# Moving a background scan forward in a two-layer kernel: first stage by K with eight output tiles, squares on ScalarE, outputs grouped by four

## The chip, the cores and the metric

The kernel runs on one core of a Trainium2 chip. The metric is the device time of one execution in microseconds (us), lower is better; the median of several executions is compared. The core has a matrix engine (TensorE, PE in the profile; PEld is its weight load), VectorE (DVE), ScalarE (ACT), GpSimd (POOL), and SyncE (SP), which issues most of the DMAs.

## The reference

Two layers run on 256 tokens of width 2048, in fp32. What the change touches lies in the first layer, which is cut to its core here:

```python
h = rmsnorm(x, norm_g)
v, bg, cg, za, u, zb, ga, gb = split(h @ w_in)      # 4 x 2048, 2 x 1024, 2 x 2048 columns
ya = (bg * causal_depthwise_conv(cg * v, conv_w) * silu(za)) @ w_out_a
yb = gelu(s5_scan(u))                               # 64 groups of 16 channels, 64 complex states each
yb = yb * sigmoid(yb @ w_glu + b_glu)
yb = (yb * silu(zb)) @ w_out_b
x1 = x + (sigmoid(ga) * ya + sigmoid(gb) * yb) @ w_o

def s5_scan(u):
    lam_bar = exp(lam * dt)                         # complex, |lam_bar| and an angle
    bu = einsum(((lam_bar - 1) / lam) * b, u)
    h[t] = lam_bar * h[t-1] + bu[t]                 # along the 256 tokens
    return real(einsum(c, h)) + d_skip * u
```

The second layer (attention beside an RWKV mix, then a gated feed-forward block) is the same in both kernels.

## The kernel before

**Matrix products.** Activations lie transposed, channels on the 128 partitions and 256 tokens along the free axis. A value that is multiplied is kept as a high part (fp32r) and a low part. `gemm` makes one output tile of 128 channels; for each block of 128 along K (a *K step*) it issues two matmuls, wh (high weights) on the high and low part together, 128x512, and wl (low weights) on the high part, 128x256. Weights come in blocks of 512 KB, one block for 8 K steps: SP loads `wf`, ACT casts `wh` (`_cast_to`), DVE subtracts `wl` (`_split_to`), each with four buffers and up to three blocks ahead (`sub`). So every 8 K steps need one `wh` on ACT and one `wl` on DVE, in whatever the stage does besides.

**Order.** The program is scheduled by hand: each engine runs its instructions in the order in which the code writes them. `gemm` calls `tick` after every K step; `tick` runs the background generators that `later` registered, and the number that a generator yields (or its default) is how many K steps pass until its next piece is written. `flush` writes out what is left of them. A time in the code is therefore a number of K steps, and a piece that is not ready when its engine comes to it stops that engine.

**Stages of the first layer, in K steps.** u takes K steps 0 to 128; the loop over f (v, cg, bg and za, four tiles for each of 16 f) goes to 1152; `ya_out`, which multiplies by `w_out_a`, to 1408; zb, ga and gb to 2048. Then the generator of the scan must be done (`flush(s5)`), and `w_glu` follows. The tile `vs` is evicted when K step 144 has ended, the first after u, and the tile `yb` is multiplied first when K step 2048 has ended.

**u.** `_block1` scales x by `norm_g` into X (ACT the high part, DVE the low part) two K blocks at a time, POOL squares x into `sq`. The first four output tiles go through K together, two K blocks per tile; the other four follow one after the other. `first_norm` adds up the squares (POOL and DVE), and `rstd` makes R, the reciprocal norm along the tokens, by a matmul with ones (`st`), some small DVE and ACT work and another matmul (`al`). `u_out` waits for R, evicts u times R, and splits it into `uh`, which goes to DRAM (`s5u`).

**The scan.** `s5` is a generator that starts after u: `s5_prep` makes small parameters (tile `sm`, mostly 128x32 on DVE and POOL), the block-diagonal matrices `bd`, and their transposes `bt` on PE; `s5_base` makes a table of the first 32 powers on POOL; and then 32 steps follow, each for two groups of channels. A step multiplies u (`bu`, two matmuls), turns it by the conjugate angles of its table (DVE products from PSUM, POOL sums), runs two real scans on DVE (line 670), turns it back (one product on POOL, one on DVE, two sums on POOL), and gives h. Beside it `s5_table` doubles the table of the next step three times (32, 64, 128 columns), one ACT and two DVE instructions each. The output y of step k is multiplied when step k+1 issues its `bu`: two fp32 matmuls of 32 output rows for the channels of that step, which go to one quarter of the bank y. After four steps y is evicted by `gelu`. In K steps, `bu` and y stand at 559, 601, 643 and so on, about 43.5 apart, to 1952, and y comes 7 K steps after the last instruction of its h.

Of the kernel before, what the change touches and what calls it, by code (L numbers as in the profile page):

```python
# [86 lines left out]
class K:  # L87
# [473 lines left out]
    def s5_base(self):  # L561
# [7 lines left out]
        for j in range(5):  # L569
# [3 lines left out]
            for i in range(2):  # L573
                self.tt(A[:, i], T[:, i, :, 0:n], pc, eng=g)
                yield 1 + j
                self.tt(B[:, 1 - i], T[:, i, :, 0:n], ps, eng=g)
                yield 1 + j
            self.tt(T[:, 0, :, n:2 * n], A[:, 0], B[:, 0], ALU.subtract, g)
            yield 1 + j
            self.tt(T[:, 1, :, n:2 * n], A[:, 1], B[:, 1], ALU.add, g)  # L580
            yield 1 + j

    def s5_table(self, k, T, w):

        base = self.flat(self.base).rearrange("p (i k t) -> p i k t", i=2, k=32)
        self.act(T[:, :, 0:32], base[:, :, k])
        for j in (5, 6, 7):
            n = 1 << j
            wv = w[:, 0:2 * n].rearrange("p (i t) -> p i t", i=2)
# [24 lines left out]
    def s5(self, U):  # L614

        nc, g = self.nc, self.nc.gpsimd
        for n in self.s5_prep():
            yield n or 9
        yield from self.s5_base()
        self.stg = self.flat(self.chunk(F32R, "stg")).rearrange("p (h i j t) -> p h i j t", h=2, i=2, j=2)  # L620
# [3 lines left out]
        two = lambda a: a[:, None, :].broadcast_to([128, 2, 256])  # L624
        ring = [c[:, 512 * i:512 * i + 512]
                for c in (self.flat(x) for x in (self.chunk(name="s5"), self.chunk(name="s5"), self.s5c)) for i in range(4)]
        m1, m2, x, s, d1, d2, w = ring[:7]
        tabs = {k: v2(ring[7 + k]) for k in range(2)}
        yield from self.s5_table(0, tabs[0], w)
        yp = {}  # L630
        for k in range(32 + 1):
            tab = iter(()) if k + 1 >= 32 else self.s5_table(k + 1, tabs[(k + 1) % 2], w)
            T, h = tabs[k % 2], ring[9 + k % 2]
            if k < 32:
                if k % 2 == 0:
# [7 lines left out]
            if k >= 1:  # L643
                a = k - 1
                q, j = divmod(a, 4)
                if j == 0:
                    yp[q] = self.pb("y")
                ha = ring[9 + a % 2]
                o = yp[q][32 * j:32 * j + 32, 0:256]
                self.mm(o, cb[:, 0, a], ha[:, 0:256], True, False)  # L650
                self.mm(o, cb[:, 1, a], ha[:, 256:512], False, True)
                if j == 3:
                    yield
                    self.later(self.gelu(q, yp.pop(q), U))
            if k == 32:
                break
            next(tab, None)
            yield
            p = v2(p[:])
            self.tt(v2(m1), p, two(T[:, 0]))  # L660
            self.tt(v2(m2), p, two(T[:, 1]))
            next(tab, None)
            yield
# [11 lines left out]
            self.tt(v2(d1), v2(s), two(T[:, 0]), eng=g)  # L675
# [3 lines left out]
            self.tt(h[:, 0:256], d1[:, 0:256], d2[:, 256:512], ALU.subtract, g)  # L679
            self.tt(h[:, 256:512], d1[:, 256:512], d2[:, 0:256], ALU.add, g)  # L680
# [14 lines left out]
    def u_out(self, p, dst, hl):  # L695
        yield from self.wait_r()
        yield from self.take(p, dst, self.R[:])
# [3 lines left out]
    def conv_out(self, f, cv, o):  # L701
        self.ts(o[:], cv[:, 0:256], self.vec("conv0", f))
# [70 lines left out]
    def _block1(self):  # L773
# [3 lines left out]
        sqs = [self.chunk(name="sq") for _ in range(2)]  # L777
# [5 lines left out]
        def scale(b):  # L783
            for k in (2 * b, 2 * b + 1):
                src = xin[k // 8][:, k % 8]
                for _ in self.scaled(X[k], src, self.vec("norm_g", k)):
                    pass
                self.tt(sqs[k // 8][:, k % 8], src, src, eng=g)

        for b in range(4):  # L790
            load(b)
# [6 lines left out]
        s, t = sqs  # L798
        self.r_ready = False

        def first_norm():
            yield 48
            for q in sqs:
                self.tt(q[:, 0:4], q[:, 0:4], q[:, 4:8], ALU.add, g)
                self.tt(q[:, 0:2], q[:, 0:2], q[:, 2:4], ALU.add, g)
            yield 16
            self.tt(s[:, 0:2], s[:, 0:2], t[:, 0:2], ALU.add)
            self.tt(self.sums[0], s[:, 0], s[:, 1], ALU.add)
            yield 6
            self.act(self.eps[:, 2:3], self.eps[:, 0:1], AF.Sqrt)  # L810
            yield 6
# [20 lines left out]
        self.s5u, self.s5b = ([self.dram.tile([128, 8, 256], F32, name=f"s5{n}{i}") for i in range(2)] for n in "ub")  # L832
# [4 lines left out]
        self.gelus = 0  # L837
        s5 = self.later(self.s5(U), ev=False, default=7)
# [724 lines left out]
def layout(a):  # L1563
# [10 lines left out]
    first = r["w_in"][:8].reshape(4, 2, 128, 4, 256)  # L1574
    r["w_in"][:8] = first.transpose(1, 3, 2, 0, 4).reshape(8, 128, 1024)
# [78 lines left out]
```

## Time and profile before

| | before |
|---|---|
| median of 3 runs | 2263.07 us (2261.43 to 2264.4) |
| profiled execution | 2257.78 us, its span 2256.0 us |
| PE busy | 2183.2 us, 97% of the span |
| DVE busy | 1714.4 us, 76% |
| ACT busy | 1093.1 us, 48% |
| POOL busy | 660.1 us, 29% |

The span goes from the first to the last instruction of the profiled execution. Busy is what an engine's own instructions cover; a busy PE may still run below its best rate. All times of rows are counted from the start of the span.

### The profile page before, as it was taken

The numbers are of one execution on the slowest core, as the hardware profiler recorded it, in microseconds if no ns is written. First come the engines' busy times: TensorE is split into PE (matmuls) and PEld (weight loads), VectorE is DVE, ScalarE is ACT, GpSimd is POOL, SyncE is SP. The second block draws the span as 40 slices with busy tenths as digits, with TensorE's granted clock in tenths as the row PEclk, the third lists the DMA queues.
The fourth block names the chain that finished last, engine by engine and source line by source line (L and its number), as shares of the span: only waits on it lengthen the run. The fifth ranks groups of instructions, "written<-read, shape, count | busy, mean of one in ns | idle before, by whom it ended". The sixth has DMA issues, their size and how long they took to land.

```text
span 2256.0 us, 37791 instructions
## 1 busy us (share of the span) xinstructions
PE 2183.2 (97%) x14500; PEld 1897.6 (84%) x14500; DVE 1714.4 (76%) x2607; ACT 1093.1 (48%) x1742; POOL 660.1 (29%) x744
## 2 busy tenths in 40 slices
PE   7999999999999999999998999999999999999997
PEld 6888777778878888899998888988888888888886
DVE  7888999988899979776797888886666555666554
ACT  5544444444445465554543454454444334444443
POOL 4345555545565312323431000411111001111111
PEclk9999999999999999999999999999999999999998
DMA  6766555557566556766546533666666666666663
GB/s 215 259 215 198 165 166 165 163 180 205 173 193 193 179 182 204 225 219 195 168 142 191 167 116 128 205 185 187 187 184 184 189 184 187 187 186 187 187 186 112
DMA packets 139537, 414.11 MB, mean 184 GB/s; under 512 B 27148, under 2 KB 43837, under 8 KB 137693
## 3 DMA queue, kind: packets, MB, share of 16 engines
q1 hardware_dynamic: 130236, 398.89, 57.2%
q0 software_dynamic: 8256, 10.49, 1.8%
q8 instruction: 114, 1.87, 0.3%
q10 hardware_dynamic: 864, 2.33, 0.3%
q14 instruction: 67, 0.54, 0.1%
HBM read 397.99 MB, written 15.75 MB: 183 GB/s over the span
## 4 chain that ended last, share of the span: by engine, by line
PE 75%; DVE 14%; DMA 3%; issue 3%; POOL 3%; ACT 1%; SPq 0%; DVEq 0%; POOLq 0%; ACTq 0%
PE acc L145 71%; DVE wl L132 5%; POOL s L132 2%; DVE s L139 2%; PE y L145 1%; DVE s L670 1%; DVE s L132 1%; ACT wh L142 1%; DMA wf<-z_in 1%; DMA a_dram<-gm 1%; DMA wf<-w_in 1%; DVE att L132 0%; DVE gb L132 0%; DVE z L132 0%; DMA gb<-a_dram 0%
## 5 line engine op out<-in xcount | busy, mean ns | idle before, releaser
L145 PE MATMUL acc<-X,wh 128*128 128x512 f32 (+1 forms) x4576 | 1397.6, 368 | 6.3 <-ACT wh L142 6.3
L132 DVE TENSOR_TENSOR wl<-wf,wh 128x1024 fp32r<-128x1024 f32 (+1 forms) x711 | 917.7, 1294 | 276.0 <-ACT wh L142 271.5
L145 PE MATMUL acc<-X,wl 128*128 128x256 f32 x3888 | 1064.9, 282 | 5.6 <-DVE wl L132 5.5
L142 ACT ACTIVATE wh<-wf 128x1024 fp32r<-128x1024 f32 (+1 forms) x711 | 748.9, 1055 | 541.6 <-PE acc L145 378.8
L145 PEld LDWEIGHTS acc<-X,wh 128*128 128x128 f32 x4576 | 811.7, 190 | 151.7 <-issue 12.8
L145 PEld LDWEIGHTS acc<-X,wl 128*128 128x128 f32 x3888 | 739.9, 190 | 27.5 <-DVE wl L132 7.5
L145 PE MATMUL acc<-s,wh 128*128 128x512 f32 (+1 forms) x726 | 246.8, 392 | 0.0
L132 POOL TENSOR_TENSOR z<-z,R 128x256 f32<-128x256 f32 x44 | 59.0, 1342 | 523.3 <-ACT sg L142 523.3
L145 PE MATMUL acc<-s,wl 128*128 128x256 f32 x704 | 192.7, 281 | 0.0
L145 PEld LDWEIGHTS acc<-s,wh 128*128 128x128 f32 x726 | 133.0, 188 | 28.9
L132 POOL TENSOR_TENSOR s<-s 128x256 f32<-128x256 f32 x128 | 114.2, 911 | 110.7 <-DVE s L132 105.1
L145 PEld LDWEIGHTS acc<-s,wl 128*128 128x128 f32 x704 | 133.0, 189 | 3.2
L132 POOL TENSOR_TENSOR sum<-sum,sq 128x256 f32<-128x256 f32 x59 | 56.1, 960 | 200.3 <-ACT sq L142 200.3
L139 DVE SCALAR_TENSOR_TENSOR s<-s,s 128x32 f32<-128x32 f32 (+2 forms) x192 | 111.9, 622 | 0.0
L142 ACT ACTIVATE z<-acc 128x256 f32<-128x256 f32 x100 | 38.2, 382 | 126.8 <-PE acc L145 126.6
L145 PE MATMUL acc<-ya,wh 128*128 128x512 f32 x256 | 90.8, 402 | 0.1
L145 PE MATMUL acc<-m,wh 128*128 128x512 f32 x256 | 89.4, 399 | 0.0
L132 DVE TENSOR_TENSOR h<-acc,h 128x256 f32<-128x256 f32 x111 | 46.9, 422 | 43.9 <-PE acc L145 41.1
L132 DVE TENSOR_TENSOR z<-acc,z 128x256 f32<-128x256 f32 x100 | 41.9, 419 | 45.2 <-ACT z L142 45.2
L132 POOL TENSOR_TENSOR bv<-bv,gs 128x128 f32<-128x128 f32 x16 | 13.3, 834 | 209.1 <-DVE bv L139 209.0
L145 PE MATMUL acc<-ya,wl 128*128 128x256 f32 x256 | 70.1, 283 | 0.4 <-ACT ya L142 0.4
L145 PE MATMUL acc<-m,wl 128*128 128x256 f32 x256 | 69.3, 281 | 0.0
(285 smaller groups left out, 2540.5 us busy)
## 6 DMA issues: line engine op xcount, KB each, us to landing
wf<-gate_up SPq DMA_DIRECT2D x176, 512.0 KB, 3.5
wf<-w_in SPq DMA_DIRECT2D x143, 512.0 KB, 4.0
wf<-down SPq DMA_DIRECT2D x88, 512.0 KB, 3.7
wf<-w_in_g SPq DMA_DIRECT2D x80, 512.0 KB, 3.7
wf<-z_in SPq DMA_DIRECT2D x54, 512.0 KB, 3.7
wf<-w_out_a SPq DMA_DIRECT2D x32, 512.0 KB, 3.9
wf<-w_o SPq DMA_DIRECT2D x32, 512.0 KB, 3.9
wf<-qk_in SPq DMA_DIRECT2D x32, 512.0 KB, 4.2
```

The costliest lines, as they stand in the source:

```text
L132: (eng or self.nc.vector).tensor_tensor(out=out, in0=a, in1=b, op=op)
L139: self.nc.vector.scalar_tensor_tensor(out=out, in0=a, scalar=s, in1=b, op0=op0, op1=op1)
L142: self.nc.scalar.activation(out=out, in_=a, func=f, **k)
L145: self.nc.tensor.matmul(out, l, r, start=start, stop=stop)
L670: nc.vector.tensor_tensor_scan(out=s[:, 256 * i:256 * i + 256], data0=r, data1=x[:, 256 * i:256 * i + 256], initial=0.0, op0=ALU.mult, op1 ...
```

## The change

1. **u by K.** All eight output tiles go through K blocks 0 to 11 together, one K step each, in eight PSUM banks; K blocks 12 to 15 then follow tile by tile. X is scaled one K block at a time. The first blocks of `w_in` are laid out for this order.
2. **Squares on ACT.** A generator makes each square on ACT and POOL adds it to `sums[0]`; the 16 squares on POOL and the trees of sums are gone. R is made later (`first_norm` waits 100 K steps).
3. **u unscaled.** `u_out` evicts u before R is there and multiplies by R in place afterwards.
4. **The scan starts in the u stage,** at K step 24 instead of 128, with 8 rather than 7 K steps between pieces, and a preparation of 4 rather than 9; after `s5_base` it waits until u is in DRAM. Its `bu` now stand at K step 279, 327 and so on, 48.25 apart, to 1774.
5. **`s5_table`** makes two products on ACT and two sums on POOL for each doubling; DVE has no part in it.
6. **Outputs by four.** h is kept in a ring of four, and `outputs` multiplies four steps at once: eight matmuls, the four quarters of the bank in turn, 24 K steps after the last instruction of the fourth h.
7. `conv_out` makes its first product on ACT instead of DVE.

The core of the diff:

```diff
     def s5_table(self, k, T, w):
-            self.act(wv, T[:, :, 0:n], scale=self.pw[:, 1, j, k:k + 1])
-            yield
-            pc = self.pw[:, 0, j, k:k + 1]
-            self.stt(T[:, 0, n:2 * n], T[:, 0, 0:n], pc, wv[:, 1], ALU.mult, ALU.subtract)
-            self.stt(T[:, 1, n:2 * n], T[:, 1, 0:n], pc, wv[:, 0], ALU.mult, ALU.add)
+            self.act(A, T[:, :, 0:n], scale=self.pw[:, 0, j, k:k + 1])
+            self.act(B, T[:, :, 0:n], scale=self.pw[:, 1, j, k:k + 1])
+            yield
+            self.tt(T[:, 0, n:2 * n], A[:, 0], B[:, 1], ALU.subtract, self.nc.gpsimd)
+            self.tt(T[:, 1, n:2 * n], A[:, 1], B[:, 0], ALU.add, self.nc.gpsimd)
             yield
...
     def s5(self, U):
         for n in self.s5_prep():
-            yield n or 9
+            yield n or 4
         yield from self.s5_base()
+        while not self.u_stored:
+            yield 1
...
+        def outputs(q):
+            y = self.pb("y")
+            for i in range(2):
+                for j in range(4):
+                    self.mm(y[32 * j:32 * j + 32, 0:256], cb[:, i, 4 * q + j], hs[j][:, 256 * i:256 * i + 256],
+                            i == 0, i == 1)
+            return y
...
-            if k >= 1:
-                a = k - 1
-                q, j = divmod(a, 4)
-                if j == 0:
-                    yp[q] = self.pb("y")
-                ha = ring[9 + a % 2]
-                o = yp[q][32 * j:32 * j + 32, 0:256]
-                self.mm(o, cb[:, 0, a], ha[:, 0:256], True, False)
-                self.mm(o, cb[:, 1, a], ha[:, 256:512], False, True)
...
+            if k and k % 4 == 0:
+                y = outputs(k // 4 - 1)
+                yield 1
+                self.later(self.gelu(k // 4 - 1, y, U))
...
     def u_out(self, p, dst, hl):
+        yield from self.take(p, dst)
+        yield
         yield from self.wait_r()
-        yield from self.take(p, dst, self.R[:])
+        self.tt(dst, dst, self.R[:])
...
     def conv_out(self, f, cv, o):
-        self.ts(o[:], cv[:, 0:256], self.vec("conv0", f))
+        self.act(o[:], cv[:, 0:256], scale=self.vec("conv0", f))
...
+        def squares():
+            for k in range(16):
+                sq = self.square(0, xin[k // 8][:, k % 8], first=k == 0)
+                yield 2
+                self.add_square(sq)
+                yield 4
...
         def first_norm():
-            yield 48
-            for q in sqs:
-                self.tt(q[:, 0:4], q[:, 0:4], q[:, 4:8], ALU.add, g)
-                self.tt(q[:, 0:2], q[:, 0:2], q[:, 2:4], ALU.add, g)
-            yield 16
-            self.tt(s[:, 0:2], s[:, 0:2], t[:, 0:2], ALU.add)
-            self.tt(self.sums[0], s[:, 0], s[:, 1], ALU.add)
-            yield 6
+            yield 100
...
-        ps = [self.acc() for _ in range(3)] + [self.pb("acc")]
-        for b in range(8):
-            if b < 5:
-                scale(b + 3)
-            part = [self.gemm(X[2 * b:2 * b + 2], p, b == 0, b == 7) for p in ps]
+        ps = [self.pb("acc") if q in (0, 2, 4, 6, 7) else self.acc() for q in range(8)]
+        self.later(squares(), ev=False)
+        for k in range(12):
+            if k + 5 < 16:
+                scale(k + 5)
+            if k == 3:
+                s5 = self.later(self.s5(U), ev=False, default=8)
+            for p in ps:
+                self.gemm(X[k:k + 1], p, k == 0, False)
         for q in range(8):
-            p = part[q] if q < 4 else self.gemm(X, self.pb("acc") if q in (4, 5) else None)
+            p = self.gemm(X[12:16], ps[q], False, True)
             self.later(self.u_out(p, U[:, q], [c[:, q] for c in uh]))
```

**PE, the outputs.** This is how PE's order of before reads where a step of the scan issues `bu` and the y of the step ahead of it (`s` is the scratch that holds h, `cbd` the matrix c); the rows around are those of a projection:

```order
L145 MATMUL acc_2380<-X_101,wl_2297 128x256
L145 MATMUL acc_2380<-X_102,wh_2316 128x512
L145 MATMUL acc_2380<-X_102,wl_2335 128x256
L145 MATMUL bu_2412<-stg_1991 128x256 x2
L145 MATMUL y_2415<-s_639,cbd_645 32x256 x2
```

In the changed kernel the y of four steps stand together, without a `bu` beside them; the first two rows of y are the four products of the real part, one for each quarter, and the next two those of the imaginary part:

```order
L145 MATMUL acc_2151<-X_99,wl_2065 128x256
L145 MATMUL y_2173<-s_1110,cbd_272 32x256
L145 MATMUL y_2173<-s_266,cbd_272 32x256 x3
L145 MATMUL y_2173<-s_1110,cbd_272 32x256
L145 MATMUL y_2173<-s_266,cbd_272 32x256 x3
L145 MATMUL acc_2151<-X_99,wh_2054 128x512
```

The y moved away from the `bu` and behind more K steps, and its neighbours now write different quarters of the bank.

**POOL, the squares.** This is the start of POOL's order before, where it squares x and adds up in trees:

```order
L132 TENSOR_TENSOR sq_98<-x_96 128x256 x8
L132 TENSOR_TENSOR sq_99<-x_97 128x256 x8
L132 TENSOR_TENSOR sq_98<-sq_98 128x1024
L132 TENSOR_TENSOR sq_98<-sq_98 128x512
L132 TENSOR_TENSOR sq_99<-sq_99 128x1024
L132 TENSOR_TENSOR sq_99<-sq_99 128x512
```

In the changed kernel the last sums of squares stand on POOL behind the small operations of `s5_prep` (`sm`, and `s` for the powers kept in a chunk of that name):

```order
L132 TENSOR_TENSOR sm_264<-s_266 128x32 x3
L132 TENSOR_TENSOR s_266<-sm_264 128x32 x2
L132 TENSOR_TENSOR sum_88<-sum_88,sq_574 128x256
L132 TENSOR_TENSOR sum_88<-sum_88,sq_600 128x256
L132 TENSOR_TENSOR sm_264<-sm_264 128x32 x8
L132 TENSOR_TENSOR sm_264<-braw_269,sm_264 128x512 x2
```

The squares left POOL, and what makes R ready there now stands in one row with the scan's preparation.

**DVE, the chain that makes R.** Before, it stands among the weights and the last scaled X, in the middle of the u stage:

```order
L132 TENSOR_TENSOR wl_429<-wf_332,wh_416 128x1024
L136 TENSOR_SCALAR rs_437<-st_426 128x2
L331 RECIPROCAL rs_437<-rs_437 128x2
L139 SCALAR_TENSOR_TENSOR rs_437<-rs_437 128x2
L132 TENSOR_TENSOR rs_437<-rs_437 128x2
L139 SCALAR_TENSOR_TENSOR rt<-rs_437 128x2
L136 TENSOR_SCALAR dg_456<-ident,rt 128x128 x2
L132 TENSOR_TENSOR wl_465<-wf_358,wh_445 128x1024
L360 COPY R<-al_455 128x256
```

In the changed kernel it stands at the end of that stage. The evictions of u (`u`), the matrices of the scan (`sm` from `braw`, `bd`), the weights (`wl`) and the chain that makes R (`rs`, `rt`, `dg`) follow one another; the second matmul of R needs the last row:

```order
L132 TENSOR_TENSOR u_159<-acc_166,u_159 128x256
L132 TENSOR_TENSOR sm_264<-braw_269,sm_264 128x512
L132 TENSOR_TENSOR u_159<-acc_167,u_159 128x256
L136 TENSOR_SCALAR rs_679<-st_668 128x2
L132 TENSOR_TENSOR bd_267<-sm_264 64x32x16 x2
L132 TENSOR_TENSOR wl_689<-wf_534,wh_672 128x1024
L132 TENSOR_TENSOR u_159<-acc_168,u_159 128x256
L331 RECIPROCAL rs_679<-rs_679 128x2
L139 SCALAR_TENSOR_TENSOR rs_679<-rs_679 128x2
L132 TENSOR_TENSOR rs_679<-rs_679 128x2
L139 SCALAR_TENSOR_TENSOR rt<-rs_679 128x2
L136 TENSOR_SCALAR dg_703<-ident,rt 128x128 x2
```

The chain moved behind work of the scan that DVE came to only in the loop over f before.

## Rows read from the trace of the kernel before

**Rows 1.** Windows by stage: us long; busy us (instructions) by engine; TensorE clock; DMA.

```profile
core 0: us, PE busy (x) PEld busy (x) DVE busy (x) ACT busy (x) POOL busy (x), PEclk, DMA share, GB/s
...
217.00:472.00 255.00, 238.93 (x1293) 196.04 (x1292) 239.61 (x351) 114.35 (x190) 129.52 (x141) 0.98 0.56 166
571.00:824.00 253.00, 246.58 (x1357) 204.62 (x1356) 225.50 (x302) 127.95 (x218) 124.09 (x135) 0.99 0.62 183
```

**Rows 2.** Tile vs: its first line, which begins when K step 144 ends.

```profile
L142 ACT ACTIVATE vs<-acc x16: 363/380/387, 69.0 to 448.9; 128x256 f32<-128x256 f32 x16
```

**Rows 3.** Tile yb: its first line, which begins when K step 2048 ends.

```profile
L145 PEld LDWEIGHTS acc<-yb,wh x64: 187/188/192, 824.1 to 846.6; 128*128 128x128 f32 x64
```

**Rows 4.** Chain of waits, its longest piece: start, us, what.

```profile
1502.32 736.38 PE acc L145 x4190
```

**Rows 5.** PE timeline around one scan step: start, us, instruction.

```profile
510.31 0.41 PE L145 MATMUL bu<-stg 96*128 96x256 f32 x2
510.64 1.05 PE L145 MATMUL y<-s,cbd 128*32 128x256 f32 x4
511.62 0.50 PE L145 MATMUL acc<-ya,wh 128*128 128x512 f32 x1
```

**Rows 6.** Waits from 217 to 824 us: us in total, times, longest.

```profile
PEld y L145 <- POOL s L132: 38.1, 39, 3.1
...
PE y L145 <- POOL s L132: 22.1, 17, 2.9
```

**Rows 7.** PE timeline of the second layer, matmuls in small tiles of the array.

```profile
1308.33 0.65 PE L145 MATMUL y<-ch,gm 64*32 64x64 f32 x32
1308.91 0.39 PE L145 MATMUL acc<-X,wh 128*128 128x256 f32 x1
```

**Rows 8.** Groups of DVE by form, 217 to 790 us: busy us, mean ns, idle before.

```profile
L670 DVE TENSOR_TENSOR_SCAN s<-s5r,s 128x256 f32<-128x256 f32 x64 | 48.2, 793 | 0.6 <-POOL s L132 0.6
L139 DVE SCALAR_TENSOR_TENSOR s<-s,s 128x128 f32<-128x128 f32 x62 | 43.5, 739 | 0.0
L132 DVE TENSOR_TENSOR s<-bu,s 128x512 f32<-128x512 f32 x64 | 41.0, 681 | 0.0
L139 DVE SCALAR_TENSOR_TENSOR s<-s,s 128x64 f32<-128x64 f32 x62 | 35.4, 610 | 0.0
L139 DVE SCALAR_TENSOR_TENSOR s<-s,s 128x32 f32<-128x32 f32 x62 | 30.5, 533 | 0.0
L132 DVE TENSOR_TENSOR s<-s,s 128x512 f32<-128x512 f32 x32 | 23.4, 732 | 0.0
```

**Rows 9.** Groups of POOL by form, 69 to 217 us, three of s5_base.

```profile
L132 POOL TENSOR_TENSOR ab<-base,s 128x128 f32<-128x128 f32 x4 | 2.6, 662 | 0.1
...
L132 POOL TENSOR_TENSOR ab<-base,s 128x32 f32<-128x32 f32 x4 | 1.2, 331 | 0.0
...
L132 POOL TENSOR_TENSOR ab<-base,s 128x64 f32<-128x64 f32 x4 | 1.1, 312 | 0.1
```

**Rows 10.** Timeline of one POOL product beside DVE, and the same product later.

```profile
489.11 3.11 POOL L132 TENSOR_TENSOR s<-s,s 128x512 f32<-128x512 f32 x1 [4.97 <-DVE s L670]
...
489.85 1.22 DVE L132 TENSOR_TENSOR wl<-wf,wh 128x1024 fp32r<-128x1024 f32 x1
...
505.01 1.39 POOL L132 TENSOR_TENSOR s<-s,s 128x512 f32<-128x512 f32 x1 [3.54 <-ACT wh L142]
```

**Rows 11.** Window of the u stage, all engines.

```profile
0.00:69.00 69.00, 57.10 (x297) 48.74 (x298) 54.33 (x86) 37.23 (x60) 25.95 (x30) 0.98 0.67 221
```

**Rows 12.** Windows of sm (DVE, POOL), bd (PE, PEld, DVE, POOL), sq (five engines); cbd's group.

```profile
60.00:217.00 157.00, 18.99 (x75) 22.05 (x51) 1.00 0.69 226
60.00:217.00 157.00, 2.40 (x16) 1.90 (x16) 3.28 (x4) 1.87 (x2) 1.00 0.69 226
0.00:69.00 69.00, 0.00 (x0) 0.00 (x0) 1.11 (x2) 0.00 (x0) 22.06 (x20) 0.98 0.67 221
...
L136 DVE TENSOR_SCALAR cbd<-cbd 128x1024 f32<-128x1024 f32 x1 | 1.2, 1250 | 0.0
```

**Rows 13.** PE's waits from 0 to 60 us: us in total, times, longest.

```profile
PE acc L145 <- DVE wl L132: 5.5, 3, 3.1
```

More of the change, by code (lines that the diff above doesn't have):

```diff
@@ L624, in s5 @@
         two = lambda a: a[:, None, :].broadcast_to([128, 2, 256])
+        s5 = [self.chunk(name="s5") for _ in range(2)]
         ring = [c[:, 512 * i:512 * i + 512]
-                for c in (self.flat(x) for x in (self.chunk(name="s5"), self.chunk(name="s5"), self.s5c)) for i in range(4)]
-        m1, m2, x, s, d1, d2, w = ring[:7]
-        tabs = {k: v2(ring[7 + k]) for k in range(2)}
-        yield from self.s5_table(0, tabs[0], w)
-        yp = {}
+                for c in (self.flat(x) for x in (s5[0], s5[1], self.s5c)) for i in range(4)]
+        m1, m2, d2 = ring[:3]
+        s, w = m1, self.flat(s5[1])[:, 0:1024]
+        tabs = {0: v2(ring[3]), 1: v2(ring[6])}
+        hs = ring[7:11]
+        yield from self.s5_table(0, tabs[0], w)
+        def outputs(q):
[5 more added lines that the diff above has]
+            return y
         for k in range(32 + 1):
             tab = iter(()) if k + 1 >= 32 else self.s5_table(k + 1, tabs[(k + 1) % 2], w)
-            T, h = tabs[k % 2], ring[9 + k % 2]
             if k < 32:
+                T, h = tabs[k % 2], hs[k % 4]
                 if k % 2 == 0:
@@ L642, in s5 @@
                     self.mm(p[:, 256 * i:256 * i + 256], st[:, 1, k % 2, 128 * i:128 * i + 128], st[:, 0, k % 2])
-            if k >= 1:
-                a = k - 1
-                q, j = divmod(a, 4)
-                if j == 0:
-                    yp[q] = self.pb("y")
-                ha = ring[9 + a % 2]
-                o = yp[q][32 * j:32 * j + 32, 0:256]
-                self.mm(o, cb[:, 0, a], ha[:, 0:256], True, False)
-                self.mm(o, cb[:, 1, a], ha[:, 256:512], False, True)
-                if j == 3:
-                    yield
-                    self.later(self.gelu(q, yp.pop(q), U))
+                next(tab, None)
+                yield
+                p = v2(p[:])
+                self.tt(v2(m1), p, two(T[:, 0]))
+                self.tt(v2(m2), p, two(T[:, 1]))
+                next(tab, None)
+            yield
[3 more added lines that the diff above has]
+                self.later(self.gelu(k // 4 - 1, y, U))
             if k == 32:
                 break
[L657 to L663, printed above, removed]
+            x = m1
             self.tt(x[:, 0:256], m1[:, 0:256], m2[:, 256:512], ALU.add, g)
@@ L674, in s5 @@
             yield
-            self.tt(v2(d1), v2(s), two(T[:, 0]), eng=g)
+            self.tt(v2(h), v2(s), two(T[:, 0]), eng=g)
             self.tt(v2(d2), v2(s), two(T[:, 1]))
@@ L776, in _block1 @@
         xin = [self.chunk(name="x") for _ in range(2)]
-        sqs = [self.chunk(name="sq") for _ in range(2)]
         X = self.hl(16, "X")
@@ L781, in load, with scale @@
             nc.sync.dma_start(out=xin[b // 4][:, 2 * (b % 4):2 * (b % 4) + 2], in_=self.i["x"][:, 2 * b:2 * b + 2])
[L783 to L788, printed above, removed]
+        def scale(k):
+            src = xin[k // 8][:, k % 8]
+            g_ = self.vec("norm_g", k)
+            self.act(X[k][0], src, scale=g_)
+            self.stt(X[k][1], src, g_, X[k][0].bitcast(F32), ALU.mult, ALU.subtract)
+        def squares():
[4 more added lines that the diff above has]
+                yield 4
         for b in range(4):
+            if b == 1:
+                self._dma_to(b)
             load(b)
@@ L836, in _block1 @@
             nc.sync.dma_start(out=self.dbg["u"], in_=U[:])
-        self.gelus = 0
-        s5 = self.later(self.s5(U), ev=False, default=7)
+        self.u_stored = True
         Ya = self.hl(16, "ya")
```

31 lines of the change are left out of this document (18 added, 13 removed).

## The prediction

> **What bounds the kernel now.** I read the windows by stage first, then the two tiles that mark where the changed stretch begins and ends, then the chain of waits, and only then single waits. PE is the bound: busy in 97% of the span, and the longest piece of the chain of waits is 4190 matmuls of PE in 736.38 us without a gap [rows 4]. Two matmuls make a K step, so an undisturbed K step costs 736.38 / 2095 = 0.3515 us.
>
> The first layer is not undisturbed. K step 144 ends at 69.0 [rows 2] and K step 2048 at 824.1 [rows 3]: 755.1 us for 1904 K steps, which alone would take 1904 x 0.3515 = 669.3. The other 85.8 us are what a change to the scan can touch. Part of them is PE's own work for the scan: around one step the `bu` starts at 510.31, the y at 510.64, and the next projection at 511.62 [rows 5], so `bu` costs 0.33 and y 0.98, and 32 steps 10.6 and 31.4; the transposes of `bd` cost 2.4 [rows 12]. The rest, 85.8 - 31.4 - 10.6 - 2.4 = 41.4, is time in which PE stood or ran slow. The table of waits names it: y waits for POOL, the last instruction of h, 22.1 us in 17 waits by the matmuls and 38.1 in 39 by their weight loads [rows 6]; the two overlap, and the longest is 3.1. No wait for `wl` stands in that stretch. The granted clock there is 0.98 to 0.99 [rows 1], which is 5 us of 255 and 3 of 253, some 10 over the whole stretch.
>
> Why is h late? DVE is busy 239.61 of 255 us in the loop over f [rows 1], so the scan's pieces queue on it and y, 7 K steps (2.5 us) after the last piece of h is written, comes too early. The step is 43.5 K steps, so this stretch holds (1152 - 559) / 43.5 = 13.6 steps of 18.7 us, of which PE needs 43.5 x 0.3515 + 1.31 = 16.6.
>
> **The change part by part.**
>
> *Outputs by four.* The same 64 fp32 matmuls are issued, but four neighbours write four quarters of the bank from four quarters of the array's columns. Before, neighbours use the same quarter, and four records take 0.98, 0.245 each. The trace has no 32-column neighbours of fp32 here; the nearest row is in the second layer, 32 small matmuls of 64 columns in 1308.91 - 1308.33 = 0.58, 18 ns each [rows 7], where 0.245 x 64 / 256 = 61 ns would be the price of one after another: 3.4 times better. 31.4 / 3.4 = 9.2, a gain of 22. Bounds: 0 if they don't overlap, 23.6 if four run as one.
>
> *The wait of y.* y now comes 24 K steps (8.4 us) after the last piece of h, 5.9 us later than before, and the longest wait was 3.1 [rows 6]; I expect it gone. What is late next is whatever follows from DVE and POOL, `wl` above all. Does DVE get relief? Six products of `s5_table` leave it, 2 x (0.739 + 0.610 + 0.533) = 3.76 us a step [rows 8], and come to POOL as six operations whose nearest rows are those of `s5_base`, 2 x (0.662 + 0.331 + 0.312) = 2.6 us [rows 9]. DVE's load of a step in the loop over f was 239.61 / 13.6 = 17.6. Of this the scan's own is 2 x 0.793 + 2 x 0.681 + 0.732 = 3.7 [rows 8], the tables 3.8 and the projections and weights 10.1 per 43.5 K steps. The new step has 48.25 K steps: 10.1 x 48.25 / 43.5 + 3.7 = 14.9, and 17.5 if each of POOL's new operations holds DVE for its whole length. PE needs 48.25 x 0.3515 + 0.33 + 0.29 = 17.6. So DVE has 2.7 us a step to spare at best and nothing at worst. Of the 41.4 I leave 12: the 10 of the lower clock and 2 of stray waits. Bounds 3 (the clock too recovers, as in [rows 4]) and 35 (most of the waits stay). The gain is 29.4.
>
> POOL and DVE do hold each other up in this trace: the product of 128x512 on POOL took 3.11 us where a `wl` of DVE stood beside it, and 1.39 later [rows 10]. The Trainium skill states the rule (SBUF — State Buffer, "Who interferes with whom"): a DVE instruction with two inputs in SBUF and a GpSimd instruction that reads SBUF take the same pair of ports, and the one that comes second is blocked wholly. By that rule what leaves DVE for POOL is no relief but for the difference of the two prices, and the step stands at the 17.5 above; the trace agrees with the blocking, not with a sum of both engines' full times. This is the page that speaks against the change, and the slower rival below is worked out from the rows.
>
> *The u stage.* Here the change costs. To K step 144 DVE was busy 54.33 of 69.0 us [rows 11]. Added are the tiles `sm` with 18.99 and `bd` with 3.28, `cbd` with 1.25; the trees of squares, 1.11, go [rows 12]: 22.4 us more on DVE before PE may pass the end of u. DVE has 14.7 us idle there. If all of it could be used the stage grows by 7.7; if none, by 22.4, and PE's stops may add 1.6. PE stops in its order at three places: `st` waits for POOL's last sums, which stand behind the small operations of `sm` (22.05 us of POOL in all, [rows 12]); `al` waits for `dg`, behind the evictions, `bd` and `wl` on DVE; and the transposes wait for banks that the evictions of u free. Behind each stands the rest of u, and then everything on PE. Against this, PE waits 5.5 us for `wl` here now [rows 13], while X is scaled two blocks at once; with one block at a time that may go, and the loss would be 7.7 - 5.5 = 2.2. I take 17: DVE's idle time of before lies mostly where data had not come (PE waited for `wl` though DVE had 14.7 to spare), so I let about 5.4 of it be used. Bounds 2 and 24.
>
> *At nothing.* The squares go from POOL, where they took 22.06 [rows 12], to ACT, which is busy 37.23 of 69 [rows 11]; `conv_out` takes a product from DVE to ACT, busy 114.35 of 255 [rows 1]; the tables give ACT three more products a step there. ACT has over half its time free to cover these; without that cover each would delay a `wh`, and so a `wl`. The transposes of `bd` (2.4) only move from one stage to the other. R's extra product on u is the same product as before. The gates of `s5` (u in DRAM, stages of `stg`) are passed once; I put 1 us for the first table on a POOL that is then busy with `s5_base`. The scan now ends some 128 K steps earlier, but its end was not waited for (last step at 1952 of 2048), so that gives nothing.
>
> *Sum.* -22.2 - 29.4 + 17 + 1 = -33.6 on the profiled execution's 2257.78, thus 2224.2. The median of the runs shown, 2263.07, is 5.3 above that execution, so the forecast for the median is 2229.
>
> **The rivals.**
>
> *B, the outputs don't overlap.* An fp32 matmul shows as two records [rows 5], and such pairs might be kept apart whatever quarter they use; nothing in the trace shows that shape. Then y keeps its 31.4: 2229 + 22 = 2251.
>
> *C, the u stage hides its new work.* For it: DVE's 14.7 of idle time and the 5.5 us of waits for `wl`. Against it: POOL's row of small operations ahead of `st`. Loss 2.2 instead of 17: 2214.
>
> *D, slower: POOL's tables and DVE block each other.* Place: the 31 steps. The one price is what the six POOL operations cost a step in blocked time. At 2.6 DVE's step is level with PE's; at the ratio of [rows 10], 3.11 / 1.39, they cost 5.8, and the step becomes 20.7 where PE needs 17.6. That is 3.1 us in each of the (1152 - 279) / 48.25 = 18 steps of the loop over f; in the 13 later ones DVE's share was 225.5 / 253 instead of 239.61 / 255 [rows 1], 0.9 us a step less, so 2.2 there: 85 us, in place of the 12 left above, 2229 + 73 = 2302. It decides where it eats the gain of 33.6 + 12 = 45.6, at 18 t + 13 (t - 0.9) = 45.6, t = 1.85, a price of 4.4 us a step. Half-way between, about 2282. Against it: six STT of DVE, which read two inputs as well, are gone.
>
> *E, the waits change their name.* y no longer waits, but `wl` comes late by as much, since PE has no other slack: 38 instead of 12 stay, 2255.
>
> **How the numbers follow.** My forecast 0.60, with a range of its own of 2214 to 2244 (the 12 between 3 and 22, the 17 between 10 and 24); B 0.10, C 0.13, D 0.10, E 0.07. A measurement of this kernel resolves about 0.2%, 4.5 us, so faster means below 2258.5. All of the forecast and of C (0.73), most of B (0.08) and half of E (0.04) lie there, 0.85; slower is nearly all of D, 0.09; what is left, 0.06, is same. The range of 8 in 10 takes in C's end and B and E, and leaves D out: 2206 (both lower bounds, 2229 - 9 - 14) to 2258.
>
> **What would show it.** Right: `vs` begins near 86 and `yb` near 790; 16 matmuls of y in about 1.2 us; no waits of y on POOL; PE's waits in the loop over f few and short; DVE's share there under 90%. The u stage is right if PE is seen to wait at `st`, `al` or the transposes. Wrong: y groups of 3.9 us (B); `vs` near 71 (C); `wl` waits of PE in the loop over f, with POOL's table operations at twice the rows above (D, E). A second layer that is not the same to within 1 or 2 us would be outside all of this.

## The result, and the profile after

The changed kernel took 2232.27 us (2228.2 to 2234.28), the kernel before 2262.25 in the runs beside it: a ratio of 0.9878, with a 95% interval of 0.9862 to 0.9893. By this ratio it is 1.2% or 27.6 us faster; the medians lie 30.0 apart, and the spans of the two profiled executions (2256.0 before, 2230.2 now) 25.8. 33.6 were forecast, and the forecast time of 2229 is off by 3.

The tile views of the changed kernel give the three marks of the first layer: `vs` begins when K step 144 has ended, `yo` 1024 K steps later, at the end of the loop over f, and `yb` when K step 2048 has ended.

```profile
L142 ACT ACTIVATE vs<-acc x16: 361/366/382, 85.8 to 457.3; 128x256 f32<-128x256 f32 x16
...
L142 ACT ACTIVATE yo<-acc x16: 362/384/387, 479.6 to 565.1; 128x256 f32<-128x256 f32 x16
...
L145 PEld LDWEIGHTS acc<-yb,wh x64: 187/188/192, 795.6 to 818.1; 128*128 128x128 f32 x64
```

Before, the first of them stood at 69.0 and the last at 824.1 [rows 2, 3]. So the u stage became 16.8 us longer, the stretch behind it 755.1 - 709.8 = 45.3 shorter, and everything behind K step 2048 took 1431.9 us before and 1434.6 here. That is 2.7 longer, outside the 1 to 2 us that the prediction allowed, but the twelve profiles of the experiments below, whose code is the same there, lie between 1428.2 and 1437.6; so no change is seen there.

In the stretch, the y of four steps takes 1.00 us, as PE's timeline shows (16 records, from 717.86 to 718.86):

```profile
717.86 1.07 PE L145 MATMUL y<-s,cbd 128*32 128x256 f32 x16
718.86 0.50 PE L145 MATMUL acc<-X,wh 128*128 128x512 f32 x1
```

Eight groups make 8.0 us where 31.4 stood, 23.4 less. Of the other 21.9, 2.4 are the transposes of `bd`, which now lie in the u stage, and 2.9 are `bu`, which costs 0.24 us (487.57 to 487.81 in PE's timeline) instead of 0.33 since y no longer follows it. The last 16.6 are waits and slow running that are gone. PE's waits of the changed kernel from 0 to 800 us name what is left:

```profile
PE acc L145 <- DVE wl L132: 18.7, 19, 3.8
PE st L145 <- POOL sum L132: 9.3, 1, 9.3
PE acc L145 <- ACT wh L142: 6.5, 1, 6.5
PE al L145 <- DVE dg L136: 2.1, 1, 2.1
PE acc L145 <- ACT ya L142: 1.0, 1, 1.0
```

No y waits for POOL any more [rows 6]; 14.5 of the 18.7 us for `wl` lie in the loop over f, where no `wl` was waited for before, and `st` and `al` stop PE in the u stage. The windows of the u stage, of most of the loop over f and of the last part of the stretch:

```profile
core 0: us, PE busy (x) PEld busy (x) DVE busy (x) ACT busy (x) POOL busy (x), PEclk, DMA share, GB/s
0.00:85.80 85.80, 63.56 (x315) 54.14 (x316) 66.66 (x160) 43.38 (x78) 37.19 (x76) 0.90 0.56 195
...
237.00:480.00 243.00, 231.61 (x1321) 194.65 (x1320) 218.64 (x267) 129.52 (x246) 195.66 (x214) 1.00 0.61 181
580.00:795.60 215.60, 215.60 (x1259) 185.83 (x1258) 181.59 (x199) 122.21 (x209) 125.86 (x132) 1.00 0.66 197
```

DVE is busy 218.64 of 243 us in the loop over f, 90% where it was 94% [rows 1]; PE is busy without a gap in the last window, 215.60 of 215.60. POOL is busy 195.66 of 243, 81%, where 129.52 of 255 stood.

### The profile page after: what moved, and what is told of

Read it like the earlier page. It is cut to its first block, busy times and chain, and to the rows that moved or that the text cites. A ratio compares the mean times of both kernels' runs of the same rounds, so it can differ in the third digit from the quotient of the medians.

```text
span 2230.2 us, 37824 instructions
## 1 busy us (share of the span) xinstructions
PE 2155.9 (97%) x14500; PEld 1888.8 (85%) x14500; DVE 1659.6 (74%) x2397; ACT 1128.2 (51%) x1870; POOL 815.1 (37%) x931
## 3 DMA queue, kind: packets, MB, share of 16 engines
q8 instruction: 114, 1.87, 0.4%
## 4 chain that ended last, share of the span: by engine, by line
PE 70%; DVE 14%; POOL 5%; issue 4%; DMA 2%; ACT 2%; SPq 0%; DVEq 0%; ACTq 0%; POOLq 0%
PE acc L145 67%; DVE wl L132 6%; POOL s L132 2%; DVE s L132 1%; DVE s L677 1%; ACT wh L142 1%; DMA wf<-z_in 1%; DVE ya L132 1%; DVE att L132 1%; POOL ab L132 1%; DMA a_dram<-gm 1%; DVE cv L132 1%; POOL ya L132 1%; DVE gb L132 1%; PE y L145 1%
## 5 line engine op out<-in xcount | busy, mean ns | idle before, releaser
L132 DVE TENSOR_TENSOR wl<-wf,wh 128x1024 fp32r<-128x1024 f32 (+1 forms) x711 | 939.2, 1326 | 283.8 <-ACT wh L142 280.0
L145 PE MATMUL acc<-X,wl 128*128 128x256 f32 x3888 | 1068.0, 283 | 18.9 <-DVE wl L132 18.7
L132 POOL TENSOR_TENSOR s<-s 128x32 f32<-128x32 f32 (+4 forms) x272 | 246.1, 924 | 43.0 <-DVE s L132 28.4
L132 POOL TENSOR_TENSOR sum<-sum,sq 128x256 f32<-128x256 f32 x74 | 70.6, 963 | 221.6 <-ACT sq L142 221.1
L132 POOL TENSOR_TENSOR s<-s,s 128x256 f32<-128x256 f32 (+1 forms) x80 | 101.2, 1281 | 24.2 <-DVE s L132 15.9
L142 ACT ACTIVATE s<-s,s 128x64 f32<-128x64 f32 (+2 forms) x192 | 69.4, 409 | 13.8 <-POOL s L132 12.2
```

Of the source, the lines that this page charges most:

```text
L132: (eng or self.nc.vector).tensor_tensor(out=out, in0=a, in1=b, op=op)
L142: self.nc.scalar.activation(out=out, in_=a, func=f, **k)
L145: self.nc.tensor.matmul(out, l, r, start=start, stop=stop)
```

## The experiments

The table holds what the chip gave: the ratio to the kernel before with its interval, and from the tile views of each profile the time at which K step 144 ended, the time of the loop over f behind it (first `vs` to first `yo`), and the whole stretch to K step 2048.

| kernel | ratio (95%) | K step 144 | loop over f | to K step 2048 |
|---|---|---|---|---|
| before | 1 | 69.0 | 408.8 | 755.1 |
| changed | 0.9878 (0.9862 to 0.9893) | 85.8 | 393.8 | 709.8 |
| after_again | 0.9866 (0.9832 to 0.9899) | 86.2 | 393.3 | 709.1 |
| y_row_by_row | 0.9894 (0.9874 to 0.9914) | 86.3 | 395.3 | 711.3 |
| y_twice | 0.9878 (0.9850 to 0.9906) | 85.6 | 393.6 | 713.2 |
| y_early | 0.9901 (0.9878 to 0.9923) | 86.6 | 397.6 | 713.8 |
| tables_on_dve | 0.9945 (0.9930 to 0.9960) | 85.7 | 403.6 | 720.8 |
| only_y | 0.9904 (0.9874 to 0.9934) | 69.0 | 404.8 | 732.9 |
| late_start | 0.9897 (0.9879 to 0.9914) | 68.6 | 399.5 | 726.9 |
| pace_7 | 0.9940 (0.9917 to 0.9962) | 85.3 | 408.0 | 722.2 |
| squares_fast | 0.9864 (0.9836 to 0.9892) | 85.7 | 393.9 | 709.9 |
| matrices_later | 0.9841 (0.9815 to 0.9867) | 76.7 | 396.2 | 712.1 |
| pace_10_7 | 0.9811 (0.9793 to 0.9829) | 76.3 | 379.5 | 704.8 |
| pace_9_8 | 0.9819 (0.9802 to 0.9835) | 77.3 | 384.4 | 703.5 |

The first repeats the changed kernel. 

> The changed kernel as it is, timed beside the next three on one chip: a ratio of 0.986 to 0.989 again. If the rest of the program is what moved, its stretch from K step 144 to 2048 would not repeat 709.8 us within 3.

It did, and the marks of the profile repeat within 0.7 us. As far as one repeat shows, differences of 2 us between profiles of this stretch can be read.

**y_row_by_row: what makes the group cheap?**

```diff
-            for i in range(2):
-                for j in range(4):
+            for j in range(4):
+                for i in range(2):
                     self.mm(y[32 * j:32 * j + 32, 0:256], cb[:, i, 4 * q + j], hs[j][:, 256 * i:256 * i + 256],
```

> The changed kernel, but the eight matmuls of a group of outputs are issued quarter by quarter, so that neighbours write the same quarter of the bank; place and delay stay. If the packing is worth what the changed kernel's trace shows (16 records in 1.00 us where before four took 0.98), a group takes 3.9 us and the time rises by 8 x 2.9 = 23 us, to about 2255. If the gain of the grouping lies in the delay alone, the time stays at 2232 within 4 us.

Neither reading held. The time hardly moved, but not because of the delay: in PE's timeline the group, now quarter by quarter, still takes 1.02 us.

```profile
719.79 1.09 PE L145 MATMUL y<-s,cbd 128*32 128x256 f32 x16
720.81 0.50 PE L145 MATMUL acc<-X,wh 128*128 128x512 f32 x1
```

**y_twice.** Each group issues its matmuls a second time, so the same sums are made twice.

```diff
-            for i in range(2):
+            for i in (0, 1, 0, 1):
                 for j in range(4):
```

> The changed kernel with the matmuls of each group of outputs issued twice over (the second pass starts the sums again), 32 records a group instead of 16. Row by row and quarter in turn took the same 1.0 us, so two readings are left. If each quarter of the array runs its own records one after the other, 0.245 us each, beside the other three quarters, a group takes 8 x 0.245 = 1.96 us and the time rises by 8 us. If the 1 us is a fixed price of going to quarters and back, whatever is done there, a group stays near 1.0 to 1.2 and the time within 3 us.

PE's timeline shows 32 records from 720.14 to 722.01:

```profile
720.14 1.93 PE L145 MATMUL y<-s,cbd 128*32 128x256 f32 x32
722.01 0.50 PE L145 MATMUL acc<-X,wh 128*128 128x512 f32 x1
```

The group takes 1.87 us, close to the 1.96 of the first reading, and no fixed price of about 1 us. The stretch grew by 3.4 to 4.1 us where the groups grew by 8 x 0.87 = 7.0; waits for `wl`, 11.4 instead of 14.5 us in the loop over f, took up most of the rest. So a quarter works through its own records at some 0.22 us each, and the four quarters do so side by side, in whichever order they were issued. Before, one quarter worked and three stood.

**y_early: does the delay of y matter?**

```diff
+            if k and k % 4 == 0:
+                y = outputs(k // 4 - 1)
+                yield 1
+                self.later(self.gelu(k // 4 - 1, y, U))
             if k < 32:
...
-            if k and k % 4 == 0:
-                y = outputs(k // 4 - 1)
-                yield 1
-                self.later(self.gelu(k // 4 - 1, y, U))
             if k == 32:
```

> The changed kernel, but a group of outputs is issued one piece (8 K steps, 2.8 us) after the last piece of the fourth h, near the place that y had before, instead of 24. Theory A (the delay took the waits away): PE waits for POOL's h at several of the eight groups, up to 3 us each, +6 to +15 us, 2238 to 2247. Theory B (h is on time since DVE is relieved): no waits of y, no change within 4 us.

Seven of the eight groups wait again, but PE's waits from 90 to 800 us show that this is mostly an exchange:

```profile
PE y L145 <- POOL s L132: 10.2, 7, 2.7
PE acc L145 <- DVE wl L132: 2.4, 3, 1.7
```

10.2 us for h came, and the waits for `wl` fell from 14.5 to 2.4. The reading is that PE waits for whichever comes last, and that `wl` catches up while PE stands at y. Neither theory holds as it stands: y waits, but the stretch is only 4.0 us longer, and the ratio is 0.0023 higher (5 us) with overlapping intervals. The delay is worth some 4 us here.

**tables_on_dve: what does the move of the tables give?** `s5_table` is that of before:

```diff
-            self.act(A, T[:, :, 0:n], scale=self.pw[:, 0, j, k:k + 1])
-            self.act(B, T[:, :, 0:n], scale=self.pw[:, 1, j, k:k + 1])
+            self.act(wv, T[:, :, 0:n], scale=self.pw[:, 1, j, k:k + 1])
             yield
-            self.tt(T[:, 0, n:2 * n], A[:, 0], B[:, 1], ALU.subtract, self.nc.gpsimd)
-            self.tt(T[:, 1, n:2 * n], A[:, 1], B[:, 0], ALU.add, self.nc.gpsimd)
+            self.stt(T[:, 0, n:2 * n], T[:, 0, 0:n], pc, wv[:, 1], ALU.mult, ALU.subtract)
+            self.stt(T[:, 1, n:2 * n], T[:, 1, 0:n], pc, wv[:, 0], ALU.mult, ALU.add)
```

> The changed kernel with s5_table as before (one ACT and two DVE instructions a doubling, nothing on POOL). Theory A, y no longer waits because it comes 24 K steps after h: no waits of y return; DVE has 3.8 us more a step and POOL some 4.5 less, so wl waits grow a little, +4 to +12 us, 2236 to 2244. Theory B, the waits went because the tables left DVE: h is late again by several us, waits of y on POOL or wl waits of 20 us and more return, 2252 or higher.

No wait of y returned, which speaks for theory A, but the waits for `wl` from 90 to 800 us are 20.7 us (14.5 in the changed kernel), which theory B named. The price lies between the two, or at the end of A's band: the ratio is 0.0067 higher, 15 us, and in the profiles the stretch grew by 11.0, 9.8 of it in the loop over f. So the tables on POOL are worth 11 to 15 us here, though POOL pays for them dearly. PE's waits from 90 to 800 us:

```profile
PE acc L145 <- DVE wl L132: 20.7, 18, 4.0
```

The three sizes in the changed kernel, groups of POOL by form from 217 to 790 us:

```profile
L132 POOL TENSOR_TENSOR s<-s 128x128 f32<-128x128 f32 x54 | 57.3, 1080 | 0.0
L132 POOL TENSOR_TENSOR s<-s 128x64 f32<-128x64 f32 x54 | 38.0, 722 | 0.3
...
L132 POOL TENSOR_TENSOR s<-s 128x32 f32<-128x32 f32 x52 | 23.4, 467 | 2.8 <-ACT s L142 2.4
```

2 x (1.080 + 0.722 + 0.467) = 4.5 us a step, where 2.6 were counted from `s5_base` [rows 9].

**only_y: the grouping by itself.** The kernel before, with `s5` of the changed kernel but its old pauses (the diff is against that `s5`); `s5_table`, `conv_out`, the u stage and the start of the scan as before.

```diff
         for n in self.s5_prep():
-            yield n or 4
+            yield n or 9
         yield from self.s5_base()
-        while not self.u_stored:
-            yield 1
```

> The kernel before with one part of the change alone, the outputs by four with their delay (and the ring of four h that it needs); u stage, start, pace of 43.5, tables on DVE and conv_out as before. If the grouping and the delay are the gain, K step 144 ends near 69, y takes 8 us instead of 31 and no longer waits, and the time falls by 23 and part of the waits, to 0.988 or lower. Rival: with tables on DVE at the old pace the waits move to wl, 20 us and more of them, and the ratio is 0.991 or higher.

0.9904: between the two. The stretch fell by 22.2 us, less than the 23.4 that y saves on PE, so no wait was saved on balance. PE's waits from 60 to 800 us:

```profile
PE acc L145 <- DVE wl L132: 23.9, 26, 2.4
PE acc L145 <- ACT ya L142: 1.7, 1, 1.7
PE y L145 <- POOL s L132: 0.2, 1, 0.2
```

The 22.1 us of y for POOL [rows 6] are gone, and 23.9 for `wl` have come. One thing besides the grouping differs: the pause before `gelu` is 1 K step here and 7 before, so with the same pauses of 7 a step takes 6 x 7 + 1/4 = 42.25 K steps instead of some 43.5. From pace_7 below (14.2 us in the loop over f for 6 K steps a step) I estimate 3 us for this, a small part of the 23.9.

**late_start: what does the early start give?** As only_y, with `s5_table` and `conv_out` of the changed kernel; so it differs from that kernel by its u stage and by

```diff
-                s5 = self.later(self.s5(U), ev=False, default=8)
+        s5 = self.later(self.s5(U), ev=False, default=7)
```

behind the u stage.

> The u stage and the start of the scan as before (squares on POOL, u four tiles at a time, scan from K step 128 with 7 K steps between pieces); outputs by four, tables on POOL and the first product of conv_out on ACT stay as in the changed kernel. If the early start costs 17 us in the u stage and gives nothing but a slower pace, K step 144 ends near 69 again and the time falls by 17 less what the pace of 43.5 instead of 48.25 K steps costs in wl waits (5 to 10 us): 2220 to 2225. Rival: the slower pace is what lets DVE and POOL keep up, and the waits come back with the old pace: 2232 or higher.

The rival came true: 2233.64 us, no faster than the changed kernel. Its marks:

```profile
L142 ACT ACTIVATE vs<-acc x16: 361/367/385, 68.6 to 442.3; 128x256 f32<-128x256 f32 x16
...
L145 PEld LDWEIGHTS acc<-yb,wh x64: 187/188/192, 795.5 to 817.9; 128*128 128x128 f32 x64
```

K step 144 ends at 68.6, 17.2 earlier, and the stretch to 2048 takes 726.9, 17.1 longer. The early start costs as much in the u stage as it gives behind it. The pace here is 42.25 K steps too, not the 43.5 of the expectation.

**pace_7: by what does it give it back?** In the changed kernel a step takes 48.25 K steps, in late_start 42.25, and the scan of the changed kernel is over 200 K steps before the stretch ends. The run has the pace of late_start; the kernel before had 43.5, not 42.25 as the expectation says.

```diff
-                s5 = self.later(self.s5(U), ev=False, default=8)
+                s5 = self.later(self.s5(U), ev=False, default=7)
```

> The changed kernel with 7 instead of 8 K steps between the pieces of the scan, so that a step takes 42.25 K steps as before, from the early start. The kernel with the late start gained 17.2 us in the u stage and lost 17.1 in the stretch from K step 144 to 2048. If the slower pace is what the early start buys, the stretch grows from 709 us to 717 to 727 here (more wl waits in the loop over f), and the total by 8 to 17 us. If it is the early end of the scan (nothing of it left in the last K steps), the stretch stays within 4 us of 709.

```profile
L142 ACT ACTIVATE vs<-acc x16: 358/366/384, 85.3 to 465.8; 128x256 f32<-128x256 f32 x16
...
L142 ACT ACTIVATE yo<-acc x16: 362/384/387, 493.3 to 578.6; 128x256 f32<-128x256 f32 x16
...
L145 PEld LDWEIGHTS acc<-yb,wh x64: 187/188/192, 807.5 to 829.9; 128*128 128x128 f32 x64
```

The stretch takes 722.2 us, 12.4 more, and all of it lies in the loop over f, 408.0 us from `vs` to `yo` and 14 more than at the slower pace; behind it pace 7 is as fast as pace 8. So 12.4 of the 17.1 us that the early start gives behind the u stage are its slower pace; the other 4.7 come from the rest of the early start, 2.4 of them from the transposes of `bd`, which left the stretch. Only part of the 14 us stands in the waits by name: they grew from 15.5 to 21.6 us. PE was busy 385.95 us in this loop instead of 378.00, at a granted clock of 0.98 instead of 1.00.

**squares_fast and matrices_later: what makes the u stage longer?**

```diff
                 self.add_square(sq)
-                yield 4
+                yield 2
```

> The changed kernel with a square every 4 K steps instead of 6, so that POOL's sums stand ahead of the scan's small operations. The wait of st for POOL's sums (9.3 us) goes. If PE then runs on, the u stage ends 9 us earlier, K step 144 near 77. Rival: DVE's work is the limit, and the next stop (al, the transposes or wl) takes most of it over: K step 144 at 81 to 86.

K step 144 stayed at 85.7. PE's waits from 0 to 90 us:

```profile
PE acc L145 <- DVE wl L132: 6.7, 4, 3.4
PE acc L145 <- ACT wh L142: 5.9, 1, 5.9
PE al L145 <- DVE dg L136: 5.1, 1, 5.1
PE st L145 <- DVE u L132: 3.5, 1, 3.5
```

`st` no longer waits for POOL's sums but 3.5 us for an eviction of u, and `al` waits longer. DVE's timeline shows who holds it:

```profile
62.63 0.72 DVE L132 TENSOR_TENSOR sm<-braw,sm 128x512 f32<-128x512 f32 x1 [4.11 <-POOL sm L132]
63.27 0.41 DVE L132 TENSOR_TENSOR u<-acc,u 128x256 f32<-128x256 f32 x1
63.61 0.14 DVE L136 TENSOR_SCALAR rs<-st 128x2 f32<-128x2 f32 x1
```

DVE stood 4.11 us at the first product with `braw`, which needs POOL's last small operations; an eviction of u and the chain of R (`rs<-st`) were ready behind it. The second kernel keeps the faster squares and moves this product and what follows from it behind the evictions of u:

```diff
         self.tt(ni, ni, d1, eng=g)
-        yield
+        yield 36
```

> The changed kernel with a square every 4 K steps, and with the scan's matrices (the products of sm with braw, bd and bt) 32 K steps later, so that DVE no longer stands before them, waiting for POOL's small operations, with the evictions of u and the chain of R behind it. If that place in DVE's order is what stops PE at st and al, K step 144 ends at 72 to 78 instead of 85.7, the stretch after it grows by up to 4 us, and the time falls by 5 to 12 us, to 0.982 to 0.985. If DVE's total work is the limit, K step 144 stays above 82 and the time as it is.

```profile
L142 ACT ACTIVATE vs<-acc x16: 358/367/384, 76.7 to 448.2; 128x256 f32<-128x256 f32 x16
```

K step 144 ends at 76.7, 9 us earlier, and `al` does not wait; the stretch behind it grew by 2.3. But the mark itself is now passed with less work done: `bd` and its transposes (2.4 us of PE) lie behind it, from 79 us on, and DVE was busy 62.21 us up to the mark, not 66.66. What the run shows without this is K step 2048, which ends at 788.8 instead of 795.6: 6.8 us from moving work without taking any away. The ratio is 0.0037 lower than that of the changed kernel (8 us), with intervals that overlap a little. So DVE's place behind POOL's small operations cost some 7 us, as far as this run shows; how much of the rest of the u stage is DVE's added work no run separates.

**pace_10_7 and pace_9_8: a slower pace in the loop over f alone.** On top of matrices_later; the second figure is the pause behind the loop.

```diff
-                s5 = self.later(self.s5(U), ev=False, default=8)
+                s5 = self.later(self.s5(U), ev=False, default=10)
...
         self.flush()
+        s5[3] = 7
         ya_out = self.dram.tile([128, 16, 256], F32, name="ya_out")
```

> The kernel matrices_later with 10 K steps between the pieces of the scan in the loop over f and 7 after it (the changed kernel has 8 throughout). The loop over f took 407.9 us at 7 and 393.8 to 396.2 at 8, while the stages after it were as fast at 7 as at 8 (93.2 and 221.1 us at 7). If pace in that loop is what makes wl late, it takes 380 to 390 us here, the rest stays, and the total falls by 6 to 15 us below matrices_later, to a ratio of 0.978 to 0.982. If the waits that are left there come from the projections alone, it stays at 394 to 396 and the ratio at 0.984.

> The same with 9 K steps in the loop over f and 8 after it. By the pace theory the loop over f lies half-way, 387 to 393 us, and the total 3 to 8 us below matrices_later; otherwise no change.

The marks of pace_10_7, and PE's waits in it from 90 to 800 us:

```profile
L142 ACT ACTIVATE vs<-acc x16: 361/367/385, 76.3 to 431.4; 128x256 f32<-128x256 f32 x16
...
L142 ACT ACTIVATE yo<-acc x16: 362/384/387, 455.8 to 540.6; 128x256 f32<-128x256 f32 x16
...
L145 PEld LDWEIGHTS acc<-yb,wh x64: 187/188/192, 781.1 to 803.5; 128*128 128x128 f32 x64
```

```profile
PE acc L145 <- DVE wl L132: 6.9, 6, 1.8
PE acc L145 <- ACT wh L142: 1.2, 1, 1.2
PE acc L145 <- ACT ya L142: 0.5, 1, 0.5
```

The loop over f takes 379.5 us at 10, 384.4 at 9, 393.3 to 396.2 at 8 and 408.0 at 7. A slower pace means fewer steps in that loop: 15 of the 32 at 10, 19 at 8, 22 at 7. At 10 the loop's waits for `wl` are nearly gone (0.8 us up to 480), and 6.1 come back behind it, where the rest of the scan is now packed closer: 325.3 us from the first `yo` to the first `yb`, instead of 315.9 in matrices_later. The expectation that the rest stays did not hold: of the 16.7 us that the loop gained over matrices_later, 7.3 are left in the whole stretch, and 8.6 with pauses of 9 and 8. Both kernels beat the changed one, with the faster squares and the later matrices included: 0.9811 (0.9793 to 0.9829) and 2215.86 us for pace_10_7, 0.9819 for pace_9_8. Their intervals overlap that of matrices_later.

## Why the prediction was right, and where not

- **Outputs by four, 22.2 us: right, 23.4.** That four neighbours must write four quarters in turn was not the reason: row by row costs the same. What counted here is that all four quarters have work at the same time.
- **The u stage, 17 us: the size right, 16.8, the working only in part.** `st` (9.3 us) and `al` (2.1) stopped PE, as the working said. PE stood 10.3 us longer in the stage than before (85.80 - 63.56 against 69.00 - 57.10), 2.4 are the transposes of `bd`, which the working had as a mere move and left out of the 17, and the last 4.1 are slower running. PE stood through the first of the windows below, from 54 to 62 us, and in the two behind it the granted clock is 0.65 and 0.79, where the whole u stage of before had 0.98 [rows 11]:

```profile
54.00:62.00 8.00, 0.00 (x0) 0.00 (x0) 4.10 (x11) 4.34 (x7) 7.92 (x26) 0.71 0.43 134
62.00:70.00 8.00, 6.02 (x20) 5.03 (x20) 5.18 (x13) 1.91 (x4) 5.38 (x10) 0.65 0.08 12
70.00:78.00 8.00, 7.80 (x41) 6.95 (x41) 7.94 (x20) 4.07 (x10) 0.00 (x0) 0.79 0.27 81
```

  The working got its 17 from DVE's added work, 22.4 us, of which 5.4 would fit into idle time. DVE's busy time grew by only 12.3 (54.33 to 66.66), and its idle time grew too, from 14.7 to 19.1. A likely reason is a term that the working put at nothing, the squares that leave POOL: a scaled X took DVE 539 ns on average where it took 877 before, and a `wl` of this stage 1259 instead of 1440 (16 and some 20 of each); in late_start, which keeps the squares on POOL, they took 877 and 1437. No run moves the squares alone. And matrices_later shows that some 7 us were DVE's order behind POOL. That the 17 was met is luck in part.
- **The waits, 41.4 to 12: mis-sized.** 709.8 - 669.3 = 40.5 stood above the bare K steps; less 8.0 for y and 32 x 0.24 = 7.7 for `bu`, 24.8 stayed instead of 12. The step that failed is "I expect it gone" as the explanation of a gain, with only "2 of stray waits" left: the later place of y took y's wait away, but in only_y some 22 us come back as waits for `wl`, and 14.5 us of such waits, 17 of them, stand in the changed kernel too, so that `yb` begins at 795.6 and not near 790. That is rival E's mechanism, and it was right for this edit; its size, 38 left, was not met in the whole change. What lowered the waits was the tables' move (11 to 15 us in the changed kernel; 6.0 from only_y to late_start, where the product of `conv_out` is in it too) and the slower pace (12.4 by pace_7). The two do not add up: together they are more than the 16.6 that went, of which PE's standing is 8.8 (24.6 to 15.8 us, from the windows of both stretches) and its slower running the rest. The pace was in the working, as 48.25 for 43.5, but the gain was booked to the delay.
- **Rival D, the blocking of DVE by POOL.** POOL's six operations take 4.5 us a step, above the 4.4 from which D should have made the kernel slower, but POOL's time is not what DVE loses. In the loop over f of tables_on_dve the six products take DVE 48.5 us (its groups by form from 85.7 to 489.3 us), yet DVE is busy only 25.7 us longer there than in the changed kernel (369.62 against 343.90). So the tables on POOL made DVE's other instructions 22.8 us longer, 1.2 us in each of 19 steps; a `wl` took 1458 ns on average instead of 1403. The mechanism is there, at about a quarter of POOL's time, and the working's upper case, each operation held for its whole length, is not what happened.
- **Rivals B and C** fell: y overlaps, and the u stage became 16.8 us longer, not 2.2.

So the nearness of the forecast is luck in part as well. Between the two profiled executions the sum was 33.6 and the gain 25.8: the waits gave 12.8 less than forecast and the part behind K step 2048 took 2.7 more, while gains that no term had (2.9 of `bu`, 2.4 of transposes that left the stretch), 1.2 more of y and 1 us for a first table that no row shows made up for half of it. The early start costs 17.2 us in the u stage and gives 17.1 behind it, so in this form it gains nothing: late_start, with the outputs by four, the tables on POOL and `conv_out` but without it, is as fast within the intervals.

## What to carry to other kernels

A background chain that shares an engine with the main chain is priced by its pace: before moving an edge of it, try how many main steps lie between its pieces, stage by stage, and read the whole stretch: of 16.7 us gained in one loop 7.3 were left, since the rest of the chain came closer together. When a wait is removed, look for what PE would have waited for next; here some 22 us came back under another name until DVE's load for each K step fell. In an in-order queue a small operation that waits for a slow engine costs what stands behind it; move the waiting instruction, not only its producer.

## What the runs showed of the hardware that was not expected

Matmuls of 32 output rows in the four quarters of the array run side by side even when they are issued quarter by quarter (16 records in 1.02 us, against 1.00 in turn), and a quarter's own records follow one another at about 0.22 us. The Trainium skill (TensorEngine Tiling (Array Packing), "Key Properties") says that different tiles can run matmuls in parallel; the runs agree, and show that the order of issue did not matter for these short groups. POOL's sums of 128x128 took 1.080 us on average beside a busy DVE, where those of `s5_base` took 0.662.

What stays open: of the 24.8 us, 15.5 are waits by name. The other 9 lie in PE's busy time in the loop over f, 378.00 us where its 1024 K steps, `bu` and y make 368.5; behind that loop nothing of the kind is left (316.0 against 316.4). No run here says what they are.
